# A two-layer trunk on one core: a sum of weights moved from VectorE into a DMA, with other buffer counts and another start

## The chip, the cores and the metric

The kernel runs on one core of a Trainium2 chip. The core has a matrix engine (TensorE, PE in the profile; its loads of the stationary operand are PEld), VectorE (DVE), ScalarE (ACT), GpSimd (POOL) and SyncE (SP), each with an instruction queue of its own that it works off in order, and 16 DMA engines that all queues share. The metric is the device time of one execution in microseconds. Of the kernel before, three runs took 2838.63, 2839.59 and 2839.4; their median is 2839.4.

## The reference, cut to what matters

The input x is 256 rows of 2048 columns, in float32, and there are two layers:

```python
for i in range(DEPTH):                      # 2
    h = rmsnorm(x, norm_mix_g[i])
    proj = h @ w_in[i]                      # GLU pair | q, k, v | forget logits | two gates
    y_conv = conformer_conv(glu_in, ...)    # GLU, causal depthwise conv of width 31, LayerNorm, swish, projection
    y_attn = forgetting_attention(q, k, v, log_f) @ w_attn_out[i]   # 8 heads of 128
    x = x + (sigmoid(g_conv) * y_conv + sigmoid(g_attn) * y_attn) @ w_out[i]
    gate, up = split(rmsnorm(x, norm_ffn_g[i]) @ w_gate_up[i])      # hidden width 5632
    x = x + (silu(gate) * up) @ w_down[i]
    x = x + sigmoid(rmsnorm(x, norm_ple_g[i]) @ w_ple_gate[i]) * (p[i] @ w_ple_proj[i])
return rmsnorm(x, final_g)
```

Nearly all of the work is products of 256 rows with weight matrices that are read once from memory.

## The kernel before, in words

**Products.** A weight tile is 128 rows by 1024 columns (two strips of 512, 512 KB). It is fetched into a `raw` buffer by SP's queue (`fetch`, L133), and `split` makes two tiles of it: `wh`, its rounded part, by ScalarE (L139), and `wl`, the rest, by VectorE (L140). TensorE multiplies three times for every strip and block of rows: rounded x with `wh`, rounded x with `wl`, the rest of x with `wh` (L178 to L180), each a matmul of 512 columns. So a plain tile is 12 matmuls. There are 7 `raw` buffers and 4 each of `wh` and `wl`.

**Fast chunks.** `fast_chunks` forms two 512-column results at once, 24 times in a layer. For one group of 512 rows of each weight matrix it uses a scheme with seven products in place of eight: it fetches four tiles a11, a21, a22, a12, VectorE adds tiles to one another (L245), and each product is 6 matmuls into one of four PSUM banks of the pool `ms` (p1, q5, q6, q7) or one of four of the pool `mm` (c11, c12, c21, c22). One of the sums, s3 = a11 + a21, has a `raw` buffer of its own, called `sum` in the trace. The other groups are plain tiles, handed out one by one by `go()`. After the product q6 the four `ms` banks are put together into u1, u4, u3, u5 (L260 to L264), and until then `state["quiet"]` holds back `run()`, which issues waiting work such as transposes (L313) and the splitting of their results (L300, L301).

**Start.** `xin` holds x, already transposed, in four pieces of four tiles. `take` scales a tile of x by a column of gains from `vecs` and splits it on ScalarE and VectorE (L303, L304). `fetch_first` brings the first weight tile in halves (L156, L160, splits at L162, L163). While these come in, `warm` issues matmuls of a tile of ones (L485).

**Attention.** For every head, `scores` adds the running sums of the forget logits to the scores by a further matmul: for the first block of 128 queries a float32 one of 128 columns (L706), for the second two of 256 columns in the type of the split operands (L710, L711).

**Order.** The program is written as straight code with queues of closures (`turns`, `tasks`, `background`). A list scheduler orders the instructions of each engine from it with its own estimates of times and with the buffers that the pools have; each engine then keeps that order.

Of the kernel before, what the change touches and what calls it, by code (L numbers as in the profile page):

```python
# [16 lines left out]
P = 128  # L17
D = 2048
S = 256
# [16 lines left out]
WARM = 10  # L36
RAWS = 7
# [8 lines left out]
def trunk(ctx, tc, xT, xR, pT, wI, wF, wC, wA, wOut, wGU, wD, wPG, wPP, vec, bF, gF, out):  # L46
# [5 lines left out]
    whs = pool("whs", 4)  # L52
    wls = pool("wls", 4)
    tmps = pool("tmps", 9)
# [13 lines left out]
    def small(n=2):  # L68
        return keep.tile([P, 16], F32, tag="small", name=f"small{next(uid)}", bufs=12)[:, :n]
# [55 lines left out]
    nsel = const.tile([P, H, P], F32R, tag="nsel", name="nsel")  # L125
# [20 lines left out]
    def fetch_first(src, hook):  # L146

        parts = []
        for half in range(2):
            raw = raws.tile([P, 2, 512], F32, tag="raw", name=f"raw{next(uid)}")  # L150
            h = whs.tile([P, 2, 512], F32R, tag="wh", name=f"wh{next(uid)}")
            l = wls.tile([P, 2, 512], F32R, tag="wl", name=f"wl{next(uid)}")
            c = half * 1024
            if half == 0:
                for k in range(2):
                    nc.scalar.dma_start(raw[:, k, :], src[:, k * 512 : (k + 1) * 512])  # L156
                warm()
                hook()
            else:
                nc.sync.dma_start(raw.rearrange("p k n -> p (k n)"), src[:, c : c + 1024])  # L160
# [53 lines left out]
    def fast_chunks(fast, w1, w2, xs, ks, first, to=None, by_block=None):  # L214
# [222 lines left out]
    def rstd_c(q):  # L437
# [14 lines left out]
        rb = keep.tile([P, S], F32, tag="rb", name=f"rb{next(uid)}", bufs=1)  # L452
# [13 lines left out]
    def take(q, lo=0, hi=4):  # L466
        for k in range(lo, hi):
            if k % 2 == 0:
                o = pair(F32R)
                norm.tiles[4 * q + k], norm.tiles[4 * q + k + 1] = o[:, 0, :], o[:, 1, :]  # L470
            norm.xs[4 * q + k] = by_blocks(norm.tiles[4 * q + k])
            halves(
                norm.tiles[4 * q + k], xin[q].rearrange("p a b -> p (a b)")[:, k * S : (k + 1) * S],
                norm.gain(4 * q + k),
            )

    load_x(0, 0, 2)
    nc.sync.dma_start(vecs[:, :KD], vec[:, :KD])
# [8 lines left out]
    def hook():  # L487
        load_x(0, 2, 4)
        take(0)
# [9 lines left out]
    def rest(q):  # L499
        def go():  # L500
            take(q)
# [18 lines left out]
    for i in range(L):  # L520
# [61 lines left out]
        wf = keep.tile([P, KD, H], F32, tag="wf", name=f"wf{next(uid)}", bufs=1)  # L582
        nc.sync.dma_start(wf, wF[i].rearrange("p (k h) -> p k h", h=H))
        wfc = keep.tile([P, KD, 2, H], F32R, tag="wfc", name=f"wfc{next(uid)}", bufs=1)
# [3 lines left out]
        ch = keep.tile([P, S], F32, tag="ch", name=f"ch{next(uid)}", bufs=1)  # L588
# [54 lines left out]
        def running_sums():  # L643
# [4 lines left out]
            act.activation(ch, pc[:, :S], AF.Copy)  # L648
            halves(chs, ch)
# [18 lines left out]
        if i == 0:  # L668
            for h in range(H):
                dve.tensor_scalar(nsel[:, h, :], ones, ident[:, h : h + 1], -1.0, op0=ALU.mult, op1=ALU.mult)  # L670
# [24 lines left out]
        def scores(hd):  # L695
            st = {}

            def sc():
                q, kt = qT[hd], kT[hd]
                pr = []  # L700
                for b in range(2):
# [3 lines left out]
                    if b == 0:  # L705
                        pe.matmul(  # L706
                            ps[:, :n], lhsT=nsel[:, hd, :].bitcast(F32), rhs=ch[:, :n], start=False, stop=True
                        )
# [180 lines left out]
        for part, nch in enumerate(FFN_PARTS):  # L889
# [32 lines left out]
            if part == len(FFN_PARTS) - 2:  # L922
                pin = keep.tile([P, 2, S], F32, tag="pin", name=f"pin{i}", bufs=1)
# [120 lines left out]
```

## Time and profile before

| | |
|---|---|
| runs | 2838.63, 2839.59, 2839.4 us |
| the profiled execution | 2838.76 us; its span, from the first to the last instruction, 2836.7 us |
| PE busy | 2816.3 us, 99% |
| VectorE busy | 2342.3 us, 83% |
| ScalarE busy | 1560.0 us, 55% |
| GpSimd busy | 9.9 us |
| moved by DMA | 543.28 MB |

A line of the profile names the source line, the engine, the operation, the tile written, the tiles read, their shape, and how many instructions are merged in it. In brackets stands how long the engine had been idle and what ended that.

### The profile page before, as it was taken

What the parts mean: (1) busy time and instruction counts of PE and PEld (TensorE: products, weight loads), DVE (VectorE), ACT (ScalarE), POOL (GpSimd) and SP (SyncE); (2) the same over time, 40 slices, a digit from 0 to 9 for tenths busy, and PEclk for the clock granted to TensorE, in tenths of its full rate; (3) what the DMA queues carried; (4) which work ended last, traced back from release to release, by engine and by line L of the source; (5) the groups of instructions that cost most, each with busy time, mean ns of one, the idle gap of its engine ahead of it and who ended that gap; (6) DMA issues with size and microseconds to landing.
All of it is one profiled execution on the core that took longest, in us unless ns stands there. A gap on an engine that the chain in (4) does not pass through costs nothing.

```text
span 2836.7 us, 34661 instructions
## 1 busy us (share of the span) xinstructions
PE 2816.3 (99%) x12744; PEld 2330.0 (82%) x12744; DVE 2342.3 (83%) x2992; ACT 1560.0 (55%) x1883; POOL 9.9 (0%) x41
## 2 busy tenths in 40 slices
PE   9999999999999999999999999999999999999998
PEld 7888888888888888888788888888888888888886
DVE  6998877868888888888869988678688888888877
ACT  6445745555555545556644466455555555455565
POOL 0000000000000000000000000000000000000000
PEclk9999999999999999999999999999999999999999
DMA  7554555565555556555555545555555556556563
GB/s 284 189 183 156 180 200 193 174 203 186 192 200 202 191 198 202 194 191 199 189 175 188 180 154 190 197 192 178 193 195 194 198 193 210 184 199 207 177 222 128
DMA packets 150074, 543.28 MB, mean 192 GB/s; under 512 B 16912, under 2 KB 17168, under 8 KB 149648
## 3 DMA queue, kind: packets, MB, share of 16 engines
q1 hardware_dynamic: 149040, 539.50, 56.3%
q8 instruction: 99, 1.62, 0.2%
q10 hardware_dynamic: 864, 1.57, 0.2%
q14 instruction: 71, 0.58, 0.1%
HBM read 538.91 MB, written 2.10 MB: 191 GB/s over the span
## 4 chain that ended last, share of the span: by engine, by line
PE 93%; DVE 5%; issue 1%; ACT 1%; DMA 0%; SPq 0%; POOLq 0%; POOL 0%; DVEq 0%; ACTq 0%
PE mm L180 27%; PE mm L179 27%; PE mm L178 27%; PE ms L178 3%; PE ms L180 3%; PE ms L179 3%; DVE wl L140 2%; DVE pair L544 2%; PE ms L313 2%; PE ms L704 0%; ACT wh L139 0%; PE ms L740 0%; DVE raw L245 0%; DMA pair<-in_xT_dram 0%; DVE pair L780 0%
## 5 line engine op out<-in xcount | busy, mean ns | idle before, releaser
L139 ACT ACTIVATE wh<-raw 128x1024 fp32r<-128x1024 f32 x1110 | 1175.9, 1061 | 1113.4 <-PE mm L180 909.5
L140 DVE TENSOR_TENSOR wl<-raw,wh 128x1024 fp32r<-128x1024 f32 x1110 | 1344.2, 1222 | 443.9 <-ACT wh L139 430.1
L178 PE MATMUL mm<-wh,pair 128*128 128x512 f32 x3552 | 1390.4, 392 | 4.2 <-ACT wh L162 2.3
L180 PE MATMUL mm<-wh,pair 128*128 128x512 f32 x3552 | 1384.4, 390 | 0.8 <-DVE pair L301 0.8
L179 PE MATMUL mm<-wl,pair 128*128 128x512 f32 x3552 | 1384.6, 390 | 0.4 <-DVE wl L140 0.3
L180 PEld LDWEIGHTS mm<-wh,pair 128*128 128x128 f32 x3552 | 667.0, 188 | 140.8 <-DVE pair L301 1.7
L178 PEld LDWEIGHTS mm<-wh,pair 128*128 128x128 f32 x3552 | 667.0, 188 | 140.0 <-ACT wh L139 2.7
L179 PEld LDWEIGHTS mm<-wl,pair 128*128 128x128 f32 x3552 | 667.7, 188 | 137.8 <-DVE wl L140 1.3
L544 DVE SCALAR_TENSOR_TENSOR pair<-pair,vecs,pair 128x256 f32<-128x256 f32 x480 | 202.7, 481 | 0.0
L245 DVE TENSOR_TENSOR raw<-raw,raw 128x1024 f32<-128x1024 f32 x144 | 175.9, 1222 | 2.7 <-DMA raw<-in_wD_dram 0.3
L178 PE MATMUL ms<-wh,pair 128*128 128x512 f32 x416 | 162.8, 391 | 1.0 <-ACT pair L975 1.0
L180 PE MATMUL ms<-wh,pair 128*128 128x512 f32 x416 | 162.0, 389 | 0.0
L179 PE MATMUL ms<-wl,pair 128*128 128x512 f32 x416 | 161.9, 389 | 0.0
L178 PEld LDWEIGHTS ms<-wh,pair 128*128 128x128 f32 x416 | 78.1, 188 | 17.9 <-ACT pair L975 1.8
L180 PEld LDWEIGHTS ms<-wh,pair 128*128 128x128 f32 x416 | 78.1, 188 | 16.3
L179 PEld LDWEIGHTS ms<-wl,pair 128*128 128x128 f32 x416 | 78.1, 188 | 16.1
L139 ACT ACTIVATE wh<-sum 128x1024 fp32r<-128x1024 f32 x48 | 50.9, 1061 | 67.0 <-PE mm L180 67.0
L140 DVE TENSOR_TENSOR wl<-sum,wh 128x1024 fp32r<-128x1024 f32 x48 | 58.6, 1220 | 11.6 <-ACT wh L139 11.6
L245 DVE TENSOR_TENSOR sum<-raw,raw 128x1024 f32<-128x1024 f32 x48 | 58.8, 1224 | 2.3 <-DMA raw<-in_wGU_dram 1.0
L288 DVE TENSOR_TENSOR tmp<-mm,tmp 128x512 f32<-128x512 f32 x80 | 51.4, 682 | 2.7 <-PE mm L180 2.7
L245 DVE TENSOR_TENSOR tmp<-tmp,mm 128x512 f32<-128x512 f32 x80 | 51.4, 680 | 0.0
L245 DVE TENSOR_TENSOR tmp<-tmp,ms 128x512 f32<-128x512 f32 x80 | 51.1, 681 | 0.0
(179 smaller groups left out, 1122.8 us busy)
## 6 DMA issues: line engine op xcount, KB each, us to landing
raw<-in_wGU_dram SPq DMA_DIRECT2D x352, 512.0 KB, 4.3
raw<-in_wI_dram SPq DMA_DIRECT2D x287, 512.0 KB, 4.0
raw<-in_wD_dram SPq DMA_DIRECT2D x176, 512.0 KB, 3.9
raw<-in_wOut_dram SPq DMA_DIRECT2D x64, 512.0 KB, 3.7
raw<-in_wPG_dram SPq DMA_DIRECT2D x64, 512.0 KB, 4.2
raw<-in_wA_dram SPq DMA_DIRECT2D x32, 512.0 KB, 4.6
raw<-in_wC_dram SPq DMA_DIRECT2D x32, 512.0 KB, 4.5
raw<-in_wPP_dram SPq DMA_DIRECT2D x8, 512.0 KB, 5.6
```

What stands on the lines that cost most here:

```text
L139: act.activation(h, raw, AF.Copy)
L140: dve.tensor_tensor(l, raw, h.bitcast(F32), op=ALU.subtract)
L178: pe.matmul(self.t, lhsT=xh, rhs=wh, start=start, stop=False)
L179: pe.matmul(self.t, lhsT=xh, rhs=wl, start=False, stop=False)
L180: pe.matmul(self.t, lhsT=xl, rhs=wh, start=False, stop=self.left == 0)
L245: add = lambda o, a, b: dve.tensor_tensor(o, a, b, op=ALU.add)
L288: dve.tensor_tensor(u, c.t, u, op=ALU.subtract)
L313: pe.transpose(pt[:, kk * S + b * P : kk * S + (b + 1) * P], src(b)[:, c : c + P], ident)
L544: dve.scalar_tensor_tensor(cv[c], u[c][:, j : j + S], w, cv[c], op0=ALU.mult, op1=ALU.add,)
```

## The change

The sum s3 is no longer formed by VectorE. SP fetches the tile a11 a second time into the buffer of s3, and GpSimd then issues a DMA that reads a21 from memory and adds it to what lies there. The four `ms` banks are put together two products and up to one plain tile later, and `quiet` ends there. `raw` has 8 buffers in place of 7, `wh` and `wl` 5 each in place of 4, `tmp` 8 in place of 9, `small` 8 in place of 12; some tiles with a buffer of their own now use a shared one. At the start the column of gains is fetched by GpSimd's queue, x comes in pieces of one, one and two tiles, `take` is called for one tile at a time ahead of each half strip of the first weight tile, and the warm-up has 20 products in place of 10. The attention scores of the first block of queries get two matmuls of 128 columns in the type of the split operands, with a broadcast column of a negated identity as the stationary operand, in place of one float32 matmul.

```diff
-WARM = 10
-RAWS = 7
+WARM = 20
+RAWS = 8
-    whs = pool("whs", 4)
-    wls = pool("wls", 4)
-    tmps = pool("tmps", 9)
+    whs = pool("whs", 5)
+    wls = pool("wls", 5)
+    tmps = pool("tmps", 8)
...
             for k in range(2):
+                take(0, 2 * half + k)
                 act.activation(h[:, k, :], raw[:, k, :], AF.Copy)
                 dve.tensor_tensor(l[:, k, :], raw[:, k, :], h[:, k, :].bitcast(F32), op=ALU.subtract)
...
             a22, a12 = fetch(w2[g][:, 1024:]), fetch(w1[g][:, 1024:])
-            s3 = raws.tile([P, 2, 512], F32, tag="raw", name=f"sum{next(uid)}")
+            s3 = fetch(w1[g][:, :1024])
+            nc.gpsimd.dma_start(s3.rearrange("p k n -> p (k n)"), w2[g][:, :1024], accum_op=ALU.add)
             product(p1, f(B11), a11)
-            add(s3, a11, a21)
             add(a21, a21, a22)
             product(q5, f(M1), a21)
             go()
             product(q7, f(T3), s3)
             add(a11, a11, a21)
             product(q6, f(T2), a11)
+            product(c21, f(N4X), a22)
+            if len(left) > 2 * len(ks):
+                go()
+            product(c11, f(B21), a12)
+            add(a12, a12, a11)
             if g == len(fast) - 1:
                 act.activation(u1, p1.t, AF.Copy)
                 dve.tensor_tensor(u4, u1, q6.t, op=ALU.subtract)
...
                 state["quiet"] = False
-                go()
-            product(c21, f(N4X), a22)
             if len(left) > 2 * len(ks):
                 go()
-            product(c11, f(B21), a12)
-            if g == 0 and len(left) > 2 * len(ks):
-                go()
-            add(a12, a12, a11)
             product(c12, f(B22), a12)
...
-    load_x(0, 0, 2)
-    nc.sync.dma_start(vecs[:, :KD], vec[:, :KD])
+    nc.gpsimd.dma_start(vecs[:, :KD], vec[:, :KD])
+    load_x(0, 0, 1)
...
     def hook():
+        load_x(0, 1, 2)
         load_x(0, 2, 4)
-        take(0)
...
-                    if b == 0:
-                        pe.matmul(
-                            ps[:, :n], lhsT=nsel[:, hd, :].bitcast(F32), rhs=ch[:, :n], start=False, stop=True
-                        )
-                    else:
-                        pe.matmul(ps[:, :S], lhsT=nsel[:, hd, :], rhs=chs[:, S:], start=False, stop=False)
-                        pe.matmul(ps[:, :S], lhsT=nsel[:, hd, :], rhs=chs[:, :S], start=False, stop=True)
+                    row = nident[:, hd : hd + 1].to_broadcast([P, P])
+                    pe.matmul(ps[:, :n], lhsT=row, rhs=chs[:, S : S + n], start=False, stop=False)
+                    pe.matmul(ps[:, :n], lhsT=row, rhs=chs[:, :n], start=False, stop=True)
```

The scheduler puts the start in another order. These are the first instructions of ScalarE before; pair_135 and pair_140 are the first four tiles of x, raw_116 and raw_149 the halves of the first weight tile, raw_184 the next one.

```order
L482 ACT_TABLE_LOAD
L482 ACTIVATE small_121<-ones 128x2 [waits Pool_49]
L303 ACTIVATE pair_135<-pair_110,vecs 128x256 [waits DMAHW3_49,DMAHW1_49]
L303 ACTIVATE pair_135<-pair_110,vecs 128x256
L303 ACTIVATE pair_140<-pair_110,vecs 128x256 [waits DMAHW4_49]
L303 ACTIVATE pair_140<-pair_110,vecs 128x256
L162 ACTIVATE wh_117<-raw_116 128x512 [waits DMAHW0_49]
L162 ACTIVATE wh_117<-raw_116 128x512 [waits DMAHW2_49]
L162 ACTIVATE wh_150<-raw_149 128x512 [waits DMAHW5_49]
L162 ACTIVATE wh_150<-raw_149 128x512
L139 ACTIVATE wh_186<-raw_184 128x1024 [waits DMAHW6_49]
```

And these are the same queue's first instructions in the changed kernel, where pair_146 and pair_159 are the first four tiles of x, raw_116 and raw_155 the halves of the first weight tile, and raw_195, raw_201 and raw_253 the three whole tiles after it.

```order
L479 ACTIVATE small_121<-ones 128x2 [waits Pool_49]
L163 ACTIVATE wh_117<-raw_116 128x512 [waits DMAHW0_49]
L163 ACTIVATE wh_117<-raw_116 128x512 [waits DMAHW3_49]
L163 ACTIVATE wh_156<-raw_155 128x512 [waits DMAHW5_49]
L163 ACTIVATE wh_156<-raw_155 128x512
L140 ACTIVATE wh_197<-raw_195 128x1024 [waits DMAHW6_49]
L665 ACTIVATE nident<-ident 128x128 [waits Pool_49]
L140 ACTIVATE wh_203<-raw_201 128x1024 [waits DMAHW7_49]
L140 ACTIVATE wh_255<-raw_253 128x1024 [waits DMAHW0_49]
L303 ACTIVATE pair_146<-pair_110,vecs 128x256 [waits DMAHW1_49,DMASW0_49]
L303 ACTIVATE pair_146<-pair_110,vecs 128x256 [waits DMAHW2_49]
```

The first tile of x has moved from ahead of the first weight split to behind the split of the fifth fetched piece of weights, raw_253.

SP's queue at the start of the kernel before, with the names as above (raw_190 and raw_242 are the weight tiles after raw_184, pair_111 the next four tiles of x):

```order
L461 DMA pair_110<-in_xT_dram 128x512
L478 DMA vecs<-in_vec_dram 128x16
L461 DMA pair_110<-in_xT_dram 128x512
L160 DMA raw_149<-in_wI_dram 128x1024
L133 DMA raw_184<-in_wI_dram 128x1024
L461 DMA pair_111<-in_xT_dram 128x1024
L133 DMA raw_190<-in_wI_dram 128x1024
L133 DMA raw_242<-in_wI_dram 128x1024
```

And in the changed kernel:

```order
L461 DMA pair_110<-in_xT_dram 128x256 x2
L461 DMA pair_110<-in_xT_dram 128x512
L160 DMA raw_155<-in_wI_dram 128x1024
L134 DMA raw_195<-in_wI_dram 128x1024
L134 DMA raw_201<-in_wI_dram 128x1024
L134 DMA raw_253<-in_wI_dram 128x1024
L134 DMA raw_259<-in_wI_dram 128x1024
L134 DMA raw_299<-in_wI_dram 128x1024
```

raw_253 stands where raw_190 stood, behind the same amount of data: the two halves of raw_116 that ScalarE's queue fetches, four tiles of x, and three pieces of 512 KB.

The third place is TensorE at the first down projection of the first part of the FFN (layer 0), where a hidden piece is transposed and used at once. Before (pair_6376 is the split transposed piece, wh_6387 the tile of c11, wh_6400 the next plain tile):

```order
L313 MATMUL ms_6379<-ident,tmp_5927 128x128
L178 MATMUL mm_6391<-wh_6387,pair_5701 128x512 [waits Activation_49]
L179 MATMUL mm_6391<-wl_6388,pair_5701 128x512
L180 MATMUL mm_6391<-wh_6387,pair_5702 128x512
L178 MATMUL mm_6391<-wh_6387,pair_5701 128x512
L179 MATMUL mm_6391<-wl_6388,pair_5701 128x512
L180 MATMUL mm_6391<-wh_6387,pair_5702 128x512
L178 MATMUL mm_6311<-wh_6400,pair_6376 128x512 [waits Activation_49]
L179 MATMUL mm_6311<-wl_6401,pair_6376 128x512
L178 MATMUL mm_6315<-wh_6400,pair_6376 128x512
L179 MATMUL mm_6315<-wl_6401,pair_6376 128x512
L180 MATMUL mm_6311<-wh_6400,pair_6376 128x512 [waits DVE_49]
```

And in the changed kernel, where pair_6423 is the split transposed piece, wh_6414 the plain tile that needs it, and wh_6480 a tile of a later step:

```order
L313 MATMUL ms_6426<-ident,tmp_5943 128x128
L313 MATMUL ms_6426<-ident,tmp_5944 128x128
L179 MATMUL mm_6371<-wh_6480,pair_6094 128x512 [waits Activation_49]
L179 MATMUL mm_6487<-wh_6480,pair_6094 128x512
L179 MATMUL mm_6330<-wh_6414,pair_6423 128x512 [waits Activation_49]
L180 MATMUL mm_6330<-wl_6415,pair_6423 128x512 [waits DVE_49]
L179 MATMUL mm_6334<-wh_6414,pair_6423 128x512
L180 MATMUL mm_6334<-wl_6415,pair_6423 128x512
L180 MATMUL mm_6371<-wl_6481,pair_6094 128x512 [waits DVE_49]
L181 MATMUL mm_6371<-wh_6480,pair_6094 128x512
L180 MATMUL mm_6487<-wl_6481,pair_6094 128x512
L181 MATMUL mm_6330<-wh_6414,pair_6423 128x512 [waits DVE_49]
```

The first use of the piece's rounded part has moved from behind six matmuls to behind two, and that of its rest (the first row that waits for VectorE on it, L180 before and L181 now) from behind ten to behind nine.

## Rows read from the trace of the kernel before

**Rows 1.** The page, busy time, share of the span and instructions by engine.

```profile
PE 2816.3 (99%) x12744; PEld 2330.0 (82%) x12744; DVE 2342.3 (83%) x2992; ACT 1560.0 (55%) x1883; POOL 9.9 (0%) x41
```

**Rows 2.** View of waits, TensorE: who was waited for, total us, times, longest.

```profile
PE mm L178 <- ACT wh L162: 2.3, 1, 2.3
PE mm L178 <- ACT wh L139: 1.8, 3, 1.2
PE ms L485 <- POOL ones L105: 1.2, 1, 1.2
PE ms L178 <- ACT pair L975: 1.0, 2, 0.5
PE mm L180 <- DVE pair L301: 0.8, 2, 0.4
PE ms L646 <- DVE lf L641: 0.5, 2, 0.2
...
```

**Rows 3.** Page, groups: busy us, mean ns, idle before and its releaser.

```profile
L139 ACT ACTIVATE wh<-raw 128x1024 fp32r<-128x1024 f32 x1110 | 1175.9, 1061 | 1113.4 <-PE mm L180 909.5
...
L245 DVE TENSOR_TENSOR sum<-raw,raw 128x1024 f32<-128x1024 f32 x48 | 58.8, 1224 | 2.3 <-DMA raw<-in_wGU_dram 1.0
```

**Rows 4.** Timeline of the start, all engines: start us, us, engine, instruction.

```profile
1.20 4.44 PE L485 MATMUL ms<-ones 128*128 128x128 f32 x20 [1.20 <-POOL ones L105]
...
5.10 0.85 SPq L133 DMA_DIRECT2D raw<-in_wI_dram  x2
5.34 0.91 ACT L303 ACTIVATE pair<-pair,vecs 128x256 fp32r<-128x256 f32 x2 [2.12 <-DMA vecs<-in_vec_dram]
...
7.30 2.18 ACT L162 ACTIVATE wh<-raw 128x512 fp32r<-128x512 f32 x4
...
7.97 0.73 PE L178 MATMUL mm<-wh,pair 128*128 128x512 f32 x2 [2.33 <-ACT wh L162]
```

**Rows 5.** DMA view of the issue at 5.10: KB, us to landing.

```profile
raw<-in_wI_dram SPq DMA_DIRECT2D x1, 512.0 KB, 8.1
```

**Rows 6.** Windows of the start: us; busy (instructions) by engine; PEclk, DMA share, GB/s.

```profile
5.00:7.00 2.00, 0.64 (x4) 0.45 (x3) 0.88 (x2) 1.42 (x4) 0.00 (x0) 1.00 1.04 374
...
9.00:12.00 3.00, 3.00 (x8) 2.32 (x8) 2.09 (x6) 1.61 (x3) 0.00 (x0) 0.50 1.00 403
```

**Rows 7.** Timeline of one fast chunk of the FFN, 826 to 848 us, several engines.

```profile
826.22 0.33 SPq L133 DMA_DIRECT2D raw<-in_wGU_dram  x1
...
828.95 1.23 DVE L245 TENSOR_TENSOR sum<-raw,raw 128x1024 f32<-128x1024 f32 x1
...
842.91 1.06 ACT L139 ACTIVATE wh<-sum 128x1024 fp32r<-128x1024 f32 x1 [1.66 <-PE mm L180]
...
847.93 0.39 PE L180 MATMUL mm<-wh,pair 128*128 128x512 f32 x1
848.16 0.39 PE L178 MATMUL ms<-wh,pair 128*128 128x512 f32 x1
```

**Rows 8.** Page: a DMA queue's packets, MB and share; DMA issues with us to landing.

```profile
q1 hardware_dynamic: 149040, 539.50, 56.3%
...
raw<-in_wGU_dram SPq DMA_DIRECT2D x352, 512.0 KB, 4.3
```

**Rows 9.** Timeline of TensorE: one head's scores, and a tile after float32 transposes.

```profile
274.69 0.39 PE L706 MATMUL ms<-ch,nsel 128*128 128x128 f32 x2
274.91 0.60 PE L704 MATMUL ms<-pair,pair 128*128 128x256 f32 x2
...
113.86 0.50 PE L178 MATMUL mm<-wh,pair 128*128 128x512 f32 x1
114.20 0.39 PE L179 MATMUL mm<-wl,pair 128*128 128x512 f32 x1
```

**Rows 10.** Groups with shapes apart: splitting a transposed tile, ScalarE's and VectorE's part.

```profile
L301 DVE TENSOR_TENSOR pair<-ms,pair 128x512 fp32r<-128x512 f32 x44 | 28.2, 683 | 0.0
...
L300 ACT ACTIVATE pair<-ms 128x512 fp32r<-128x512 f32 x44 | 23.7, 583 | 1.0 <-PE mm L179 1.0
```

More of the change, by code (lines that the diff above doesn't have):

```diff
@@ L68, in small @@
     def small(n=2):
-        return keep.tile([P, 16], F32, tag="small", name=f"small{next(uid)}", bufs=12)[:, :n]
+        return keep.tile([P, 16], F32, tag="small", name=f"small{next(uid)}", bufs=8)[:, :n]
     def bank_mm():
@@ L124, in trunk @@
     )
-    nsel = const.tile([P, H, P], F32R, tag="nsel", name="nsel")
+    nident = const.tile([P, P], F32R, tag="nident", name="nident")
     lf = const.tile([P, 2, P], F32, tag="lf", name="lf")
@@ L152, in fetch_first @@
             l = wls.tile([P, 2, 512], F32R, tag="wl", name=f"wl{next(uid)}")
-            c = half * 1024
             if half == 0:
@@ L159, in fetch_first @@
             else:
-                nc.sync.dma_start(raw.rearrange("p k n -> p (k n)"), src[:, c : c + 1024])
+                nc.sync.dma_start(raw.rearrange("p k n -> p (k n)"), src[:, 1024:])
             for k in range(2):
+                take(0, 2 * half + k)
                 act.activation(h[:, k, :], raw[:, k, :], AF.Copy)
@@ L451, in rstd_c @@
         pe.matmul(ps2[:, :S], lhsT=ones, rhs=dg[:, :S], start=True, stop=True)
-        rb = keep.tile([P, S], F32, tag="rb", name=f"rb{next(uid)}", bufs=1)
+        rb = keep.tile([P, S], F32, tag="lsum", name=f"rb{next(uid)}", bufs=1)
         act.activation(rb, ps2[:, :S], AF.Copy)
@@ L464, in load_x, with take @@
         )
[L466 to L474, printed above, removed]
-            )
-    load_x(0, 0, 2)
-    nc.sync.dma_start(vecs[:, :KD], vec[:, :KD])
+    def take(q, k):
+        if k % 2 == 0:
+            o = pair(F32R)
+            norm.tiles[4 * q + k], norm.tiles[4 * q + k + 1] = o[:, 0, :], o[:, 1, :]
+        to = norm.tiles[4 * q + k]
+        halves(to, xin[q].rearrange("p a b -> p (a b)")[:, k * S : (k + 1) * S], norm.gain(4 * q + k))
+        norm.xs[4 * q + k] = by_blocks(to)
+    nc.gpsimd.dma_start(vecs[:, :KD], vec[:, :KD])
+    load_x(0, 0, 1)
     def warm():
@@ L500, in go @@
         def go():
-            take(q)
+            for k in range(4):
+                take(q, k)
             load_x(q + 1) if q < 3 else None
@@ L579, in trunk @@
             turns.append(lambda hh=hh, at=at: conv_in(hh, at))
-        wf = keep.tile([P, KD, H], F32, tag="wf", name=f"wf{next(uid)}", bufs=1)
+        wf = tmps.tile([P, KD, H], F32, tag="tmp", name=f"wf{next(uid)}")
         nc.sync.dma_start(wf, wF[i].rearrange("p (k h) -> p k h", h=H))
-        wfc = keep.tile([P, KD, 2, H], F32R, tag="wfc", name=f"wfc{next(uid)}", bufs=1)
+        wfc = tmps.tile([P, KD, 2, H], F32R, tag="tmp", name=f"wfc{next(uid)}")
         act.activation(wfc[:, :, 0, :], wf, AF.Copy)
@@ L587, in trunk @@
         fls = tmp()
-        ch = keep.tile([P, S], F32, tag="ch", name=f"ch{next(uid)}", bufs=1)
         chs = keep.tile([P, 512], F32R, tag="chs", name=f"chs{next(uid)}", bufs=1)
@@ L647, in running_sums @@
             pe.matmul(pc[:, P:S], lhsT=lf[:, 1, :], rhs=upper[:, :P], start=False, stop=True)
-            act.activation(ch, pc[:, :S], AF.Copy)
-            halves(chs, ch)
+            halves(chs, pc[:, :S])
             pt0 = bank_ms()
@@ L668, in trunk @@
         if i == 0:
-            for h in range(H):
-                dve.tensor_scalar(nsel[:, h, :], ones, ident[:, h : h + 1], -1.0, op0=ALU.mult, op1=ALU.mult)
+            act.activation(nident, ident, AF.Copy, scale=-1.0)
         rq = keep.tile([P, 2], F32, tag="rq", name=f"rq{next(uid)}", bufs=1)
@@ L704, in sc @@
                     pe.matmul(ps[:, :n], lhsT=q[:, b * P : n], rhs=kt[:, :n], start=True, stop=False)
-                    if b == 0:
-                        pe.matmul(
-                            ps[:, :n], lhsT=nsel[:, hd, :].bitcast(F32), rhs=ch[:, :n], start=False, stop=True
-                        )
-                    else:
-                        pe.matmul(ps[:, :S], lhsT=nsel[:, hd, :], rhs=chs[:, S:], start=False, stop=False)
-                        pe.matmul(ps[:, :S], lhsT=nsel[:, hd, :], rhs=chs[:, :S], start=False, stop=True)
+                    row = nident[:, hd : hd + 1].to_broadcast([P, P])
+                    pe.matmul(ps[:, :n], lhsT=row, rhs=chs[:, S : S + n], start=False, stop=False)
+                    pe.matmul(ps[:, :n], lhsT=row, rhs=chs[:, :n], start=False, stop=True)
                     t = tmp()
@@ L922, in trunk @@
             if part == len(FFN_PARTS) - 2:
-                pin = keep.tile([P, 2, S], F32, tag="pin", name=f"pin{i}", bufs=1)
+                pin = tmp().rearrange("p (k s) -> p k s", k=2)
                 nc.sync.dma_start(pin, pT[i])
```

## The prediction

> **What bounds the kernel now.** I read the busy times first: TensorE is busy 2816.3 of a span of 2836.7 us, VectorE 83% and ScalarE 55% [rows 1]. Then who TensorE waits for: the reader is to see how little there is. The rows add to 7.6 us, of which 2.3 and 1.2 lie at the start; 1.8, 1.0, 0.8 and 0.5, together 4.1, lie in all the rest [rows 2]. Third, the groups: ScalarE's splits stood idle 909.5 us until TensorE gave a buffer back, so the engines that prepare weights run ahead of TensorE and wait for it [rows 3]. Last, the start: TensorE warms up from 1.20 to 5.64, stands still, and begins real work at 7.97 [rows 4]. From there on it is a nearly unbroken row of matmuls, so a change of time can come from four places only: the moment of the first matmul, the 4.1 us of waits, new waits, and matmuls that are added or replaced.
>
> **The start.** The changed order decides here. ScalarE works off its queue in order, and in the changed kernel the first tile of x (pair_146) stands behind the split of raw_253; the first real matmul needs that tile. raw_253 takes the place in SP's queue that raw_190 had, behind the same bytes, and its issue waits as that one's did for the first fetch of ScalarE's queue to land. Before, raw_190 was issued at 5.10 [rows 4] and landed 8.1 us later [rows 5], at 13.2. The DMA engines were fully busy meanwhile, share 1.00 from 9 to 12 [rows 6], so fetching x in smaller pieces won't bring it sooner. Add its split, 1.06 [rows 3], and one scaling of x, half of 0.91 = 0.46 [rows 4]: the first real matmul comes at 13.2 + 1.06 + 0.46 = 14.7, where it came at 7.97. That is 6.8 us later (14.72 to 14.77, with the few hundredths that a signal takes). What TensorE then finds is ready: five pieces of weights are split already, and the later tiles of x follow one another at 0.46 on ScalarE, faster than the 12 matmuls that use a pair. So the shift is neither regained nor added to.
>
> The longer warm-up: 20 records took 4.44 us, 0.22 each [rows 4]; 40 take 8.9 at that pace and end at 10.1, or sooner when the clock rises on the way. Either way they are over well before 14.7 and cost nothing themselves. [...]
>
> VectorE's eight products for the old selection tiles go, and ScalarE gets one small copy instead (nident); it stands between splits that wait for fetches, and costs nothing.
>
> **The sum by DMA.** VectorE loses 48 sums of 1.22 us, 58.8 us in all [rows 3]. VectorE is not what TensorE waits for except in a few of the 4.1 us, so this is not 58.8 us of time. Added are 48 fetches and 48 adding DMAs of 512 KB, 50 MB beside 539.5 MB that take 56.3% of the DMA engines [rows 8]: about 62%, still no bound. The new chain is fetch, adding DMA, split, product. In one fast chunk: SP issued the last of the four fetches at 826.22, when a buffer came free; the sum, in the next free one, was made at 828.95, its split began at 842.91 and TensorE reached its product at 848.16 [rows 7]. With an eighth buffer the fetch for the sum gets the release that the fourth fetch had, so it is issued at 826.2 or sooner and lands 4.3 later [rows 8], at 830.5. To be in time for TensorE the split has to begin 1.06 + 1.22 ahead of 848.16, at 845.9. So the adding DMA may take 15.4 us from release to landing before TensorE notices. No row shows one. The nearest are the plain fetches of the same size, 4.3 in the steady part and 8.1 at the crowded start [rows 8, 5]; I take the time as between these, hidden, at nothing. The bounds: it can't gain anything but VectorE's share above, and beyond 15.4 every further microsecond costs 48.
>
> [...]
>
> GpSimd was busy 9.9 us [rows 1], so the adding DMAs, which wait on its queue for their fetches, hold up only a handful of small powers for the norms behind them; these are needed half a fast chunk later at the earliest. Cost nothing; if one were late it would be by one fetch, 4.3.
>
> **More buffers and results put together later.** A fifth pair of split buffers lets the splits run one tile further ahead. It and the lighter VectorE can take away at most the 4.1 us; some of these do not hang on buffers (the forget logits' 0.5, the copies that free PSUM banks, 1.0), so I take half, 2.05. Against that, putting the four banks together later holds back the transposes of the last hidden piece. Where a product of the down projection needs it at once, in the first part of the FFN of each layer, the changed order has two matmuls in place of six between the transposes and the use of the rounded part, and nine in place of ten before the rest is used. The split of a half takes 0.58 on ScalarE and then 0.68 on VectorE [rows 10]; the rest came 0.4 late before [rows 2] and now has one matmul, 0.23, less: 0.5 more for the two layers. Between nothing and a whole split each time, 2 x 1.26 = 2.5. Fewer `tmp` and `small` buffers: the order of the changed kernel keeps tiles moving between their uses, nothing; at worst they eat the other half, 2.05.
>
> **The heads.** 16 times a float32 matmul of 128 columns goes; it takes 274.91 - 274.69 = 0.22 [rows 9]. Two of 128 columns in the other type come. At the spacing of the wide ones, 848.16 - 847.93 = 0.23 for 512 columns [rows 7], they take 0.06 each, a gain of 0.10 a head, 1.7 in all; if such narrow ones are as slow as float32, a loss of 0.22, 3.5 in all. The first of that type behind a float32 one had 0.34 in place of 0.23 [rows 9], which gives 0.11 a head back, 1.8. I take 0, between -1.7 and +5.3.
>
> **The sum.** +6.8 (start) + 0 (sum by DMA) - 2.05 (waits) + 0.5 (transposes) + 0 (heads) = +5.25. The profiled execution took 2838.76, so 2844.0; it lies within the three runs before, whose median is 2839.4, and against that 2844.0 is +4.6 or 0.16%. A measurement of this kernel can tell about 0.2% from no change, 5.7 us, so the point lies just inside no change, on its slow side.
>
> **Rivals.**
> 1. The adding DMA is late. For it: it queues behind fetches, its own fetch among them, and no row shows one. Against it: 15.4 us of slack. At four times the plain 4.3 it takes 17.2 and is 1.8 late, 48 x 1.8 = 86 us: about 2930. It decides from 15.4 on, and makes the kernel slower.
> 2. The start costs more and nothing comes back: 6.8, 2 for a second low stretch of the clock, 0.5, and 3.5 for slow narrow matmuls, 12.8: 2851.6. For it: the longer standstill of TensorE. Against it: before, the clock was back 4 us after the first matmul.
> 3. The start costs less. If raw_253 lands at the pace that the engines had from 9 to 12, 403 GB/s [rows 6], the 3.15 MB up to it take 7.8 us from 2 on, and the first matmul comes at 11.3, 3.3 late; with all 4.1 of waits gone the time is 2838.0, no change. For it: the bytes would allow it. Against it: raw_190 did not land so. A full clock on top (-2) makes it 2836. To be measurably faster the kernel needs more than all the waits that the trace has; only with the clock and matmuls cheaper too.
>
> **How the numbers follow.** Forecast, 70%: its own range is 2840 to 2848, from the start (an earlier or later landing by 1), the waits (0 to 4.1 back) and the heads; 45 of the 70 lie under 2845.1, the bound of no change, 25 above. Rival 1, 6%; rival 2, 12%; rival 3, 10%, of it 8 no change and 2 faster; 2% for something faster that I don't see. Faster 0.04, no change 0.53, slower 0.43. The range 2839 to 2851.5 leaves out rival 1, half of rival 2 and most of rival 3.
>
> **What would show it.** Start: the first real matmul at 14.7, released by a scaling of x on ScalarE, which stands behind a split that waited for a fetch; the granted clock 0.50 for some microseconds after it. Sum by DMA: landings under 15 us, and no wait of TensorE or ScalarE for the sum's buffer. Waits: the rows of TensorE outside the start adding to 1 to 4 us, with the one for L301 not gone. Heads: starts of the two narrow matmuls 0.06 or 0.22 apart. I am wrong if real work begins before 11 or after 17, if a row "DMA" stands among ScalarE's longest waits, or if TensorE's waits outside the start grow above 8.

## The result, and the profile after

The changed kernel takes 2846.25 us (2844.57 to 2847.37) where the kernel before, on the same chip, takes 2839.48: a ratio of 1.0025, interval 1.0015 to 1.0034. It is 6.8 us slower; 2844.0 was forecast, with 2839.0 to 2851.5 as range. The two profiled executions stand 7.2 apart (2845.96 and 2838.76), their spans 7.6.

TensorE's busy time and its waits, the rows that answer to [rows 1] and [rows 2]:

```profile
PE 2819.1 (99%) x12764; PEld 2332.1 (82%) x12764; DVE 2283.8 (80%) x2936; ACT 1553.9 (55%) x1882; POOL 52.0 (2%) x90
```

```profile
PE mm L179 <- ACT pair L303: 6.3, 1, 6.3
PE mm L179 <- ACT wh L140: 1.5, 2, 0.8
PE ms L482 <- POOL ones L105: 1.2, 1, 1.2
PE ms L313 <- DVE xt L935: 1.0, 1, 1.0
PE mm L179 <- ACT pair L300: 0.7, 2, 0.3
PE ms L719 <- DVE tmp L712: 0.7, 1, 0.7
PE ms L313 <- DVE xt L862: 0.5, 2, 0.3
PE ms L643 <- DVE lf L638: 0.4, 2, 0.2
PE ms L179 <- ACT pair L966: 0.4, 1, 0.4
```

One wait of 6.3 at the start stands out. The rest, without the first and the 1.2 of the warm-up, add to 5.2. The like sum of the kernel before is 4.6: the 4.1 of [rows 2] and two more rows of the same view, which the prediction did not count:

```profile
PE mm L179 <- DVE wl L140: 0.3, 1, 0.3
PE ms L313 <- DVE xt L944: 0.2, 1, 0.2
```

VectorE lost 58.5 us of work and TensorE's waits did not shrink. Two new ones, 0.75 each, are for splits (L140).

The start, against [rows 4]: TensorE, then ScalarE's queue (start us, us):

```profile
1.20 6.48 PE L482 MATMUL ms<-ones 128*128 128x128 f32 x40 [1.20 <-POOL ones L105]
13.95 0.79 PE L179 MATMUL mm<-wh,pair 128*128 128x512 f32 x1 [6.27 <-ACT pair L303]
```

```profile
8.67 1.15 ACT L163 ACTIVATE wh<-raw 128x512 fp32r<-128x512 f32 x2 [2.13 <-DMA raw<-in_wI_dram]
9.96 1.06 ACT L140 ACTIVATE wh<-raw 128x1024 fp32r<-128x1024 f32 x1
10.92 0.29 ACT L665 ACTIVATE nident<-ident 128x128 fp32r<-128x128 f32 x1
11.20 1.06 ACT L140 ACTIVATE wh<-raw 128x1024 fp32r<-128x1024 f32 x1
12.44 1.06 ACT L140 ACTIVATE wh<-raw 128x1024 fp32r<-128x1024 f32 x1 [0.18 <-DMA raw<-in_wI_dram]
13.41 1.69 ACT L303 ACTIVATE pair<-pair,vecs 128x256 fp32r<-128x256 f32 x4
```

The scaling of x (L303) stands behind three whole splits, the third of which waited for its fetch; TensorE begins 0.5 after it. The windows after the standstill, as [rows 6] (PEclk is the third number from the end): the clock falls to 0.50, where wide matmuls start 0.43 apart (16.23, 16.65, 17.08), and is nearly back in 18 to 20, where they start 0.23 apart (18.68, 18.91). The last line is from the kernel before, where the clock was nearly back in 12 to 15.

```profile
9.00:12.00 3.00, 0.00 (x0) 0.00 (x0) 2.24 (x3) 2.85 (x5) 0.00 (x0) 0.95 1.03 423
12.00:15.00 3.00, 1.05 (x2) 0.50 (x2) 2.97 (x4) 2.82 (x6) 0.00 (x0) 0.50 1.02 416
15.00:18.00 3.00, 2.96 (x8) 2.24 (x8) 1.34 (x4) 0.10 (x1) 0.00 (x0) 0.50 1.02 419
18.00:20.00 2.00, 2.00 (x9) 1.65 (x8) 0.00 (x0) 0.65 (x1) 0.00 (x0) 0.86 1.03 422
```

```profile
12.00:15.00 3.00, 3.00 (x15) 2.48 (x14) 3.00 (x8) 3.00 (x6) 0.00 (x0) 0.98 1.04 426
```

Read in slices of 0.2 us, the clock is low for 3.4 us before (8.7 to 12.1) and for 6.8 us now (11.7 to 18.6); 4.6 of these 6.8 come after the first real matmul.

The adding DMAs, against [rows 8]: their queue is q0; for wGU a landing takes 7.6 in the median where a plain fetch now takes 4.6.

```profile
q1 hardware_dynamic: 155952, 564.66, 59.1%
q0 software_dynamic: 6944, 25.18, 5.0%
...
raw<-in_wGU_dram SPq DMA_DIRECT2D x372, 512.0 KB, 4.6
...
raw<-in_wGU_dram POOLq DMA_DIRECT2D x20, 512.0 KB, 7.6
```

The view of the tile that they write, all 48 together, says who waited for it: ScalarE, 4 times, all in the FFN.

```profile
  ACT wh L140: 9.3, 4
...
DMA to landing us min/median/max: 5.1/7.5/9.8
```

One head's scores, as [rows 9]:

```profile
283.39 0.38 PE L699 MATMUL ms<-pair,pair 128*128 128x128 f32 x2
283.53 0.31 PE L701 MATMUL ms<-chs,nident 128*128 128x128 f32 x1
283.67 0.28 PE L702 MATMUL ms<-chs,nident 128*128 128x128 f32 x1
283.78 0.65 PE L699 MATMUL ms<-pair,pair 128*128 128x256 f32 x2
...
284.50 0.39 PE L179 MATMUL mm<-wh,pair 128*128 128x512 f32 x1
```

From 283.39 to the next product at 284.50 are 1.11 us. The narrow matmul that ends a pair takes 0.11, the one before it 0.14.

### The profile page after: what moved, and what is told of

It is laid out like the page before. It is cut to its first block, busy times and chain, and to the rows that moved or that the text cites. A ratio compares the mean times of both kernels' runs of the same rounds, so it can differ in the third digit from the quotient of the medians.

```text
span 2844.3 us, 34899 instructions
## 1 busy us (share of the span) xinstructions
PE 2819.1 (99%) x12764; PEld 2332.1 (82%) x12764; DVE 2283.8 (80%) x2936; ACT 1553.9 (55%) x1882; POOL 52.0 (2%) x90
## 4 chain that ended last, share of the span: by engine, by line
PE 91%; DVE 6%; DMA 1%; issue 1%; ACT 1%; SPq 0%; POOLq 0%; POOL 0%; DVEq 0%; ACTq 0%
PE mm L181 26%; PE mm L179 26%; PE mm L180 26%; PE ms L179 3%; PE ms L181 3%; PE ms L180 3%; DVE wl L141 2%; DVE pair L542 2%; PE ms L313 2%; DMA raw<-in_wI_dram 1%; ACT wh L140 0%; DMA raw<-in_wD_dram 0%; PE ms L699 0%; DMA raw<-in_wOut_dram 0%; PE ms L731 0%
## 5 line engine op out<-in xcount | busy, mean ns | idle before, releaser
L140 ACT ACTIVATE wh<-raw 128x1024 fp32r<-128x1024 f32 x1158 | 1220.1, 1060 | 1169.0 <-PE mm L181 918.5
L141 DVE TENSOR_TENSOR wl<-raw,wh 128x1024 fp32r<-128x1024 f32 x1158 | 1396.6, 1221 | 467.6 <-ACT wh L140 462.5
L179 PE MATMUL mm<-wh,pair 128*128 128x512 f32 x3552 | 1392.5, 392 | 8.7 <-ACT pair L303 6.3
L181 PE MATMUL mm<-wh,pair 128*128 128x512 f32 x3552 | 1384.4, 390 | 0.0
L180 PE MATMUL mm<-wl,pair 128*128 128x512 f32 x3552 | 1383.9, 390 | 0.0
L179 PEld LDWEIGHTS mm<-wh,pair 128*128 128x128 f32 x3552 | 667.4, 188 | 145.8 <-ACT pair L303 6.5
L181 PEld LDWEIGHTS mm<-wh,pair 128*128 128x128 f32 x3552 | 667.2, 188 | 140.5 <-DVE pair L304 0.8
L180 PEld LDWEIGHTS mm<-wl,pair 128*128 128x128 f32 x3552 | 667.8, 188 | 135.5
L179 PE MATMUL ms<-wh,pair 128*128 128x512 f32 x416 | 162.9, 392 | 0.4 <-ACT pair L966 0.4
L180 PE MATMUL ms<-wl,pair 128*128 128x512 f32 x416 | 162.0, 389 | 0.0
L181 PE MATMUL ms<-wh,pair 128*128 128x512 f32 x416 | 161.9, 389 | 0.0
L179 PEld LDWEIGHTS ms<-wh,pair 128*128 128x128 f32 x416 | 78.1, 188 | 17.6 <-ACT pair L966 1.5
L181 PEld LDWEIGHTS ms<-wh,pair 128*128 128x128 f32 x416 | 78.1, 188 | 16.3
L180 PEld LDWEIGHTS ms<-wl,pair 128*128 128x128 f32 x416 | 78.1, 188 | 16.0
L399 ACT ACTIVATE tmp<-xt 128x512 f32<-128x512 f32 x56 | 34.8, 623 | 15.2 <-DVE xt L862 7.9
L862 DVE TENSOR_TENSOR xt<-xt,tmp 128x512 f32<-128x512 f32 x64 | 41.1, 684 | 0.0
L301 DVE TENSOR_TENSOR pair<-ms,pair 128x512 fp32r<-128x512 f32 (+1 forms) x60 | 34.9, 612 | 1.1 <-ACT pair L300 1.1
```

What stands on the lines that cost most here:

```text
L140: act.activation(h, raw, AF.Copy)
L141: dve.tensor_tensor(l, raw, h.bitcast(F32), op=ALU.subtract)
L179: pe.matmul(self.t, lhsT=xh, rhs=wh, start=start, stop=False)
L180: pe.matmul(self.t, lhsT=xh, rhs=wl, start=False, stop=False)
L181: pe.matmul(self.t, lhsT=xl, rhs=wh, start=False, stop=self.left == 0)
L301: dve.tensor_tensor(lo, src, hi.bitcast(F32), op=ALU.subtract)
```

## The experiments

They were timed in three sets of four, each set on one chip beside the kernel before (its medians: 2839.29, 2838.9, 2838.84); the third set (b_start_sp, e_best, e_best_late_old, e_four_bufs) ran on another chip than the first two. e_two_adds has 4 executions and e_four_bufs 5, the others 11. The columns behind the time are from the profiled execution: the start of the first real matmul, then how much later than before the 96th of the wide matmuls (512 columns, L179 to L181) starts, and how much further behind the last of them is. The second tells what the start costs, the third what all the rest does; one execution's third column can be off by 1 or more. Five kernels have all of the change except its start (after, e_old_start, e_order, e_vecs_sp, e_vecs_sp_warm10): theirs runs from -0.4 to +1.0. The profiled executions of b_start_sp and e_best are the fastest of their eleven.

```
kernel             us       ratio, interval           first   96th   rest
before             2839.48                             7.97
after              2846.25  1.0025 1.0015-1.0034      13.95   +6.5   +1.0
b_new_start        2845.47  1.0023 1.0014-1.0031      12.44   +7.3   +0.1
e_old_start        2838.79  1.0000 0.9991-1.0009       8.14   +0.2   -0.4
e_order            2842.31  1.0010 1.0001-1.0019      10.62   +3.1   +1.0
e_vecs_sp          2837.28  0.9995 0.9986-1.0003       8.16   -1.3   +0.2
e_vecs_sp_warm10   2836.56  0.9991 0.9982-1.0000       6.08   -2.0   +0.5
b_start_sp         2837.19  0.9994 0.9986-1.0003       5.84   -3.3   -0.1
e_sum_dve          2835.57  0.9988 0.9979-0.9997       8.38   -1.4   -0.5
e_late_old         2838.29  0.9998 0.9989-1.0006       7.52   -1.8   +1.7
e_best             2834.92  0.9987 0.9978-0.9996       5.70   -2.1   -2.3
e_best_late_old    2836.33  0.9990 0.9981-0.9999       5.63   -1.9   -1.7
e_four_bufs        2850.87  1.0040 1.0027-1.0053       7.48   -2.2  +13.3
e_two_adds         2951.47  1.0391 1.0375-1.0407       8.56   -1.3   +117
```

**The start alone, and everything but the start.** In the kernel before: the new `take`, the loads and the warm-up (b_new_start). In the changed kernel, the reverse:

```
e_old_start:  WARM = 10;  load_x(0, 0, 2);  nc.sync.dma_start(vecs[:, :KD], ...)
              hook(): load_x(0, 2, 4); all four take(0, k)
```

> The kernel before with the new start alone (40 warm-up matmuls, x in smaller pieces taken one by one, vecs by GpSimd's queue); sums by VectorE, buffers, heads and the time of putting results together as before. With four split buffers the first tile of x stands behind a split one earlier in SP's queue than in the changed kernel. Theory: first matmul at 12.5 to 13.5, the kernel 4.5 to 6 us slower than before, 2844 to 2845.5. Rival (the late start needs the adding DMAs or the fifth buffers): first matmul near 8, within 1 us of the kernel before.

> The changed kernel with the whole start of the kernel before (20 warm-up records, x in its old pieces, all four tiles of the first quarter scaled at once, vecs on SP); the rest of the change stays: adding DMAs, buffers, results put together later, heads. Theory (of the 7.5 us that the last matmul is late, 6.5 come from the start and about 1 from the rest): within 1.5 us of the kernel before, 2839.5 to 2841. Rival (the rest of the change regains the 2 us forecast, and something else eats it at the start): under 2838.5. Rival (the rest costs several us by itself): above 2842.

The new start alone costs 6.2 us, the changed kernel without it stands where the kernel before does. Its 2838.79 lies below the range of the theory of e_old_start, which gave the rest about 1 us: no cost of the rest shows. In b_new_start ScalarE's queue shows the same picture one split earlier (four split buffers), and the first matmul follows at 12.44; then TensorE is held up once more, 1.6, and its clock is low from 13.9 to 20.7, all of it after the first matmul, so its 96th matmul is no earlier than the changed kernel's:

```profile
9.73 2.26 ACT L139 ACTIVATE wh<-raw 128x1024 fp32r<-128x1024 f32 x2 [0.23 <-DMA raw<-in_wI_dram]
11.89 1.69 ACT L304 ACTIVATE pair<-pair,vecs 128x256 fp32r<-128x256 f32 x4
```

**What in the start.** Moving one small DMA moves both the landing of the gains and ScalarE's order. Two kernels part them:

```
e_order:    + dependence without a semaphore: both halves of x's first tile
              (L303) -> split of raw_195
e_vecs_sp:  -    nc.gpsimd.dma_start(vecs[:, :KD], vec[:, :KD])
                 load_x(0, 0, 1)
            +    nc.sync.dma_start(vecs[:, :KD], vec[:, :KD])
```

> The changed kernel with one thing forced in ScalarE's queue: the two halves of the first tile of x (pair_146, pair_159) stand ahead of the split of raw_195, as a dependence without a semaphore; vecs still come by GpSimd's queue. It parts the two things that the fetch of vecs changed: when the gains land, and where the scaling of x stands in ScalarE's order. In the changed kernel vecs were issued at 2.89 and took 6.4, so the gains are there at 9.3. Theory (the place in the order costs most): first real matmul at 9.3 + 0.46 and a few hundredths, 9.8, some 1.8 later than in the kernel before and 4.1 earlier than in the changed one; the clock falls after it as before; the time is 2841 to 2842.5. Rival (the gains' way through GpSimd's queue is the cause, the order only follows from it): first matmul after 12, the time above 2844.

> The changed kernel, with one DMA put back: the first gains (vecs) are fetched by SP's queue behind the first piece of x, not by GpSimd's. Everything else of the change stays, the 40 warm-up matmuls too. In its order ScalarE scales the first tile of x ahead of the splits again. Theory (the start is late because the first tile of x stands behind a split in ScalarE's queue): the first real matmul comes at 7.5 to 8.5 instead of 13.95, the time falls by some 6 us to about 2840. Rival A (the start is late because of the bytes in front of raw_253 or because x comes in smaller pieces): the first matmul stays later than 11 and the time stays above 2843. Rival B (with 40 warm-up matmuls the clock now stays up, since hardly any standstill is left): the low stretch after the first matmul goes as well, another 2 us or so, about 2838.

> As e_vecs_sp, with 20 warm-up matmul records in place of 40. It tells what the longer warm-up is worth once TensorE does not stand still after it. Theory (the longer warm-up is worth something only when real work follows it at once): TensorE stands still for 2 us before the first matmul, the clock is low after it as in the kernel before, and the time is some 2 us above e_vecs_sp. Rival (the warm-up's length is worth nothing): the same time as e_vecs_sp within 0.5 us.

Both count. With the gains still on GpSimd's queue the new order alone lets e_order begin 3.3 us sooner, of the 5.8 between the changed kernel and e_vecs_sp, and it takes 3.9 us less, of 9.0. The first matmul came at 10.62, not 9.8, for two reasons that were not in the expectation: the gains landed at 9.74, not 9.3, and the tile now stood behind the splits of a piece that landed at 8.79.

```profile
8.82 1.15 ACT L172 ACTIVATE wh<-raw 128x512 fp32r<-128x512 f32 x2 [1.99 <-DMA raw<-in_wI_dram]
...
10.07 1.70 ACT L312 ACTIVATE pair<-pair,vecs 128x256 fp32r<-128x256 f32 x4
```

With the gains on SP's queue ScalarE takes x and the first pieces in turn, from 4.79 on, and the 9.0 us come back. TensorE, which has nothing to wait for after its warm-up, now keeps its clock:

```profile
1.21 7.20 PE L482 MATMUL ms<-ones 128*128 128x128 f32 x40 [1.21 <-POOL ones L105]
8.16 0.48 PE L179 MATMUL mm<-wh,pair 128*128 128x512 f32 x1
```

```profile
9.00:12.00 3.00, 2.88 (x13) 2.07 (x12) 1.78 (x4) 1.84 (x4) 0.00 (x0) 1.00 1.03 411
```

By its 11th wide matmul it is 1.65 ahead of before, though its first one was 0.2 later. Here rival B of the expectation holds. What the 40 warm-up matmuls did for it the next kernel tells: with 20, real work begins at 6.08, the standstill is 0.6, and the clock stays up as well; the time is 0.7 lower, within scatter. The longer warm-up is not needed, the theory that it is worth 2 us fell, and where x is ready it stands in the way of real work.

```profile
1.21 4.28 PE L482 MATMUL ms<-ones 128*128 128x128 f32 x20 [1.21 <-POOL ones L105]
6.08 0.73 PE L179 MATMUL mm<-wh,pair 128*128 128x512 f32 x2 [0.60 <-ACT wh L163]
```

```profile
9.00:12.00 3.00, 2.30 (x9) 1.38 (x8) 1.83 (x4) 2.51 (x5) 0.00 (x0) 1.00 1.02 416
```

The kernel before with this mended start and nothing else (new `take` and loads, vecs on SP, WARM = 10):

> The kernel before with the new start alone, as b_new_start, but vecs by SP's queue and 20 warm-up records. It gives the worth of taking the first tiles one by one by itself. Theory: first real matmul near 6.1 as in e_vecs_sp_warm10, no low stretch of the clock, 2 us or a little more under the kernel before, about 2837. Rival (the gain needs the rest of the change): within 0.7 of the kernel before.

As the theory had it: 2837.19, 1.7 under the kernel before of its set. Its interval reaches 1.0003, so the time alone does not show the gain. In the trace every wide matmul from the 24th to the last is 3.3 to 3.4 earlier than before, but that execution, 2835.36, is the fastest of eleven: taking the tiles one by one very likely pays by itself, by 1.7 to 3.4.

**The sum by DMA.** Made by VectorE again, or the adding DMA issued twice:

```
e_sum_dve:  -  s3 = fetch(w1[g][:, :1024]);  nc.gpsimd.dma_start(s3, w2..., accum_op=ALU.add)
            +  s3 = raws.tile(...);  add(s3, a11, a21)    # behind product(p1, ...)
e_two_adds: the line with accum_op=ALU.add stands twice
```

> As e_vecs_sp, but the sum of each group is made by VectorE from the two pieces that are there anyway, as in the kernel before: no adding DMA, no extra fetch, 50 MB less traffic. Theory (VectorE's 58.8 us lie off the path, and the adding DMA is hidden): the same time as e_vecs_sp within 1 us, 2836.3 to 2838.3, with the same waits of TensorE in the two places where it waits for L140. Rival A (the lighter VectorE is worth some of TensorE's waits): 1 to 2 us slower, 2838.5 to 2839.5, with waits for VectorE's tiles up. Rival B (the 50 MB or the late sum cost something): 1 us or more faster, under 2836.3.

> As e_vecs_sp, but each adding DMA is issued twice, one behind the other, so that the sum is a + 2b in place of a + b: another 25 MB, and the sum lands one adding DMA later. It measures the slack that hides the sum. In the changed kernel a fetch of wGU took 4.6, the issue of the adding DMA 0.85 and its landing 7.6: 13.1 from release, 2.3 under the 15.4 that the trace of before gave. Theory (15.4 from release to landing, then 48 us per us): 13.1 + 0.85 + 7.6 = 21.5, 6.1 late, 48 x 6.1 = 293 slower, about 3130. Rival (the pieces behind the sum in the queue run further ahead, or TensorE's stalls give back lead, so that only a part of it is seen): 20 to 200 us slower. Rival (the slack is larger than read): no change, 2837.

Without the adding DMA the kernel is 1.7 faster (rival B), and the second pair, e_best against e_vecs_sp_warm10, gives 1.6. The intervals overlap, each difference by itself is not resolved; that both pairs agree makes a small cost likely. Where it arises stays open: no wait of TensorE's names the sum.

A third comparison goes against "nothing to gain". e_best and b_start_sp, of one set, have the same start; e_best has the rest of the change too, without the adding DMA, and takes 2.3 us less. That is about the size of the 2.05 that the prediction hoped to get back, again with intervals that overlap.

Twice the DMA costs 114, within the first rival's 20 to 200. The waits for a sum's tile on ScalarE, 9.0 in e_vecs_sp, are now:

```profile
  ACT wh L140: 239.4, 37
...
DMA to landing us min/median/max: 5.2/7.6/10.1
```

The theory fell in two places. TensorE lost nearly all of it in the output projection and the FFN: in the first layer its wide matmuls fall 6.7 behind over the 2 sums of wOut and 50 over the FFN's 16, so some 3.1 to 3.4 each in the mean, not 6.1; by the end of wI's sums it is where e_vecs_sp is. Not all of the 114 is waiting. TensorE's waits outside the start grow by 73 us (77.6 against 4.9). The rest is in good part the clock: behind many of these waits it is 0.50, for 61 us in all, counted in slices of 1 us and without the end of the kernel, where it is low too (for the last 8.6 in the kernel before, 9.8 in the changed one); at half speed that is 31 us, as an estimate. And in one such chunk the first DMA was issued at 850.78 and ScalarE's wait for the second ended at 867.15:

```profile
850.78 0.84 POOL L252 DMA_DIRECT2D raw<-in_wGU_dram  x1 [36.84 <-DVE wl L141]
858.50 0.86 POOL L253 DMA_DIRECT2D raw<-in_wGU_dram  x1 [6.87 <-DMA raw<-in_wGU_dram]
```

```profile
867.15 2.95 ACT L140 ACTIVATE wh<-raw 128x1024 fp32r<-128x1024 f32 x3 [9.25 <-DMA raw<-in_wGU_dram]
```

That is 16.4 from issue to split. TensorE then waits three times, 3.4 in all, and runs at the low clock for a while:

```profile
874.00:878.00 4.00, 4.00 (x12) 3.13 (x11) 3.97 (x5) 0.10 (x1) 0.00 (x0) 0.57 0.59 190
```

Over this chunk it falls 5.9 behind e_vecs_sp. The clock's part is 1.7 (3.4 us at half speed), so the split came some 4.2 too late: here the sum may take about 12.2 from its issue and takes 7.6 in the median, a spare of 4.6. The chunks differ: the one whose first DMA was issued at 945.25 had its split 15.5 later and lost 0.3. So the spare is some 4 to 8 us, as an estimate from two chunks, where 15.4 - 13.1 = 2.3 had been read.

**Buffers, and when results are put together.**

```
e_four_bufs: whs and wls 5 -> 4 (from e_vecs_sp)
e_late_old:  u1, u4, u2, u3, u5 and go() ahead of product(c21, ...), as before (from e_vecs_sp)
e_best:      e_sum_dve with WARM = 10;  e_best_late_old: e_best with the order of e_late_old
```

> As e_vecs_sp, with four pairs of split buffers in place of five. Theory (TensorE's few waits don't hang on these buffers): the time of e_vecs_sp, 2837.3, within 0.7, with the same rows of waits. Rival (the fifth pair hides the late sums): waits of TensorE for L141 or L140 in the fast chunks, and 1 to 5 us slower.

> As e_vecs_sp, but the four banks of a group of sums are put together where the kernel before did it, ahead of the products c21 and c11, with the transposes called there as before. The changed kernel has a new wait of 0.75 for a split at 309.8 and at 1720.9, and the row of matmuls falls 1.4 to 1.8 behind between the 1092nd and the 1392nd. Theory (putting together later causes it): both waits are gone, the time falls by 1 to 1.5 us, to about 2836. Rival (it comes from the adding DMA, the buffers or the heads): the waits are there still, the time is that of e_vecs_sp within 0.5 us. Against both: moving it back brings up other waits for VectorE's copies, and the time rises by up to 1 us.

> As e_vecs_sp_warm10 (vecs by SP's queue, 20 warm-up records), and the sums made by VectorE again as in e_sum_dve: what the runs so far point to as the best. It is also a second, paired look at the price of the adding DMA. Theory (the adding DMA and its 50 MB cost something small): 1 to 2 us under e_vecs_sp_warm10's 2836.6, about 2835. Rival (the 1.7 us between e_vecs_sp and e_sum_dve were scatter): 2836 to 2837.

> As e_best, with the banks of a group of sums put together where the kernel before did it: a second look at what putting together later is worth, without the adding DMA. Theory (it only moves TensorE's waits: 1.5 for L140 and some for VectorE's tiles with it, others for the turned pieces' xt without it): within 1 us of e_best, the two waits of 0.8 for L140 gone, those for xt up by about as much. Rival (it is worth what e_late_old lost, 1.0): 1 us or more above e_best.

e_four_bufs is the surprise: 13.6 slower than e_vecs_sp, which ran on another chip (14.0 when each is taken against the kernel before of its set), above even the rival's 5. Its waits of TensorE, which add to 14.1 without the warm-up's where e_vecs_sp has 4.9:

```profile
PE mm L179 <- ACT wh L140: 6.0, 9, 1.3
PE ms L313 <- DVE xt L862: 3.1, 4, 1.1
PE ms L179 <- ACT pair L966: 2.1, 3, 1.1
...
PE ms L313 <- DVE xt L935: 1.1, 1, 1.1
PE ms L719 <- DVE tmp L712: 0.9, 1, 0.9
```

Of the 12.2 between the two spans they make up 9.2; what makes up the rest was not followed. They are waits for splits and for turned pieces, not for L141 of a sum, and ScalarE waits for an adding DMA's tile once only, 2.7:

```profile
  ACT wh L140: 2.7, 1
```

So the fifth pair is what the rest of the change lives on: the kernel before, and b_start_sp, have four pairs and lose nothing of the kind. No wait names the sums as what it covers. Whether the later putting together, the DMAs' place among the fetches, the heads or the smaller pools need it was not tried.

Putting together later does cause the two new waits for L140: in e_late_old and in e_best_late_old they are gone. But others for xt take their place,

```profile
PE ms L314 <- DVE xt L863: 2.4, 6, 0.7
PE ms L314 <- DVE xt L936: 1.7, 1, 1.7
```

and the time rises by 1.0 and 1.4 in the two pairs: within scatter, but not the gain that the theory of e_late_old promised. In the second pair the waits for xt do not rise so far (0.9 in all), and the 1.4 is the rival's size.

e_best, 2834.92, ratio 0.9987 (0.9978 to 0.9996), beats both kernels: 11 us under the changed one (on another chip), 4 under the one before, which is 0.13%.

## Why the prediction was right, point by point

- **The start, +6.8.** Right in mechanism, and in size partly by luck: the landing came earlier than forecast, and the clock, which has no term in the sum, took 0.5 of that back. The split ahead of x waited for its fetch, which was issued at 4.86 instead of 5.10 and landed by 12.44 instead of 13.2, so the first matmul came at 13.95, 6.0 late, not at 14.7. In the first ten matmuls these 6.0 grew to 6.5, by the clock, and stayed so. b_new_start, 6.2 slower, shows it alone. The prediction took the order as given; that the fetch of the gains by GpSimd had brought it about, and that one line undoes it, only the runs showed.
- **The clock.** The sign came, 0.50 after the first matmul. No run shows the 2 us that rival 2 puts on a second low stretch and rival 3 takes off for a full clock. What the runs showed in its place: the low stretch lasts 6.8 us in place of 3.4. The 40 warm-up records were over in 6.48, at a granted clock of 1.00 all along, sooner than the 8.9 at the pace of the 20. The low stretch began while TensorE stood still, so only 4.6 us of it fall on real work, 1.2 more than before, and cost the 0.5 above. Not seen was how near the other side lay: in e_vecs_sp and with 20 records and a standstill of 0.6 it stays up. That is worth about 1.4: e_vecs_sp and e_old_start begin at 8.16 and 8.14, and are 1.3 ahead and 0.2 behind by the 96th matmul (1.25 and 0.19).
- **The sum by DMA, 0.** Right that it is hidden: rival 1 did not come. The landing of 7.6 lies between the 4.3 and 8.1 taken as bounds. The slack was read too small, and the cost is rather 1.6 than nothing, if two unresolved pairs are believed. The sign "no wait of ScalarE for the sum's buffer" did not hold: ScalarE waited 4 times, 9.3 us in all, though no wait of TensorE followed from it. The longest of the 48 landings took 9.8.
- **The waits, -2.05.** This step failed. Nothing was regained: the waits outside the start went from 4.6 to 5.2, and in e_old_start, with the same rest, they are 4.0. The step asked what a fifth pair of buffers and a lighter VectorE could take away, and took the rest of the change as asking nothing of them. e_four_bufs shows the pair paying for 13.6 us that the rest would cost, and e_late_old shows waits giving way to others. Without the adding DMA (e_best against b_start_sp) some 2 us may come back.
- **Transposes, +0.5.** Not seen. Where the last hidden piece is turned, the 0.40 that TensorE waited for the rest of the split (L301, VectorE) [rows 2] went, and 0.34 for its rounded part (L300, ScalarE) came in its place, twice each: the part that the order brought nearer became the later one, and the price was nothing. What putting together later cost lies elsewhere: the two waits of 0.75 for L140.
- **Heads, 0.** Right: 1.11 from the first score to the next product in both ([rows 9] for the matmuls before; 274.47 to 275.58). The narrow ones take 0.11 to 0.14, between the 0.06 and 0.22 of the bounds.
- **The sum.** Start 0.3 too high, the rest -1.55 instead of +1.0 in the profiled execution: 2.6 too low. By e_old_start the rest is nearer to nothing, so between 1 and 2.6 too low. 2844.0 lay 2.25 under the measured 2846.25. Of the signs named ahead, these came: x on ScalarE behind a split that waited, landings under 15, no wait of TensorE for the sum's tile. These did not: no wait of ScalarE for that tile, waits of TensorE of 1 to 4 (5.2), and narrow matmuls 0.06 or 0.22 apart (0.11 and 0.14).

## What to carry to other kernels

Where an engine works its queue in order, look in the new order for the first instruction that the bottleneck needs and for what stands ahead of it: here the route of an 8 KB fetch moved it behind the splits of the first five pieces of weights and cost 9.0 us, where the waits that the rest of the change could remove are 4.6. A buffer added in the same change as new latencies may be paying for them: remove it alone before counting it as gain. When the bottleneck is 99% busy, work taken from another engine is worth no more than the waits that name that engine: here those that name VectorE were 1.8 us, and 58.5 us of work taken from it made nothing shorter.

## What the runs showed of the chip that was not expected

- An adding DMA of 512 KB from GpSimd's queue took 5.1 to 9.8 us to land, median 7.5, where plain fetches of the same size from SP's queue took 3.8 to 6.1 (medians by weight matrix); issuing one took GpSimd 0.84 to 0.89. Whether the adding or the queue makes it longer was not tried. A second one onto the same tile took no longer than the first (medians 7.2 and 8.0 in e_two_adds).
- The granted clock stayed at 1.00 with a standstill of 0.6 us or none behind the warm-up, with 20 matmul records as with 40; it fell after standstills of 2.3 (e_old_start), 2.9 (e_order), 3.7 (b_new_start) and 6.3 us (the changed kernel). It was then low for 3.4 us in the first two and for 6.8 in the last two. In e_best_late_old it stayed up through a wait of 1.3 among the first real matmuls.
- The clock also fell in mid-kernel: in e_two_adds waits of 0.6, 0.8 and 2.0 close together were followed by 3.4 us at 0.50, and such stretches cost about 31 of the 114 us, as an estimate.
